# The samples' second small product of a pair is put behind the next pair's sums, in the same PSUM bank

## The chip, the cores and the metric

The kernel runs on one core of one Trainium2 chip. The metric is the device time in microseconds (us) of one execution; lower is better. Three runs of the kernel before the change gave 816.17, 815.36 and 816.26 us, median 816.17 us.

The core's engines run side by side, each through its own list of instructions in order, and wait for each other by semaphores: PE (TensorE, matrix products; its loading of weights is shown as PEld), DVE (VectorE), ACT (ScalarE), POOL (GpSimd), and SP, which only issues DMAs. [...]

## The reference, cut to what matters

One inference step of a hybrid decoder layer: 1024 prompt positions and 8 x 4 = 32 sample positions go through the same weights. `h @ w_in` gives the queries, keys, values and gates of two branches, an mLSTM and a sliding-window attention; these are gated, projected, summed, projected by `w_o` and normalised.

```python
h, gate = adaln_in(x, c, w_ada, b_ada, g_norm)
(mq, mk, mv, mi, mf, mo, mz, aq, ak, av, az, gm, ga) = split_in(h @ w_in)
y_m, C, n, m = mlstm_branch(mq, mk, mv, mi, mf, mo, mz, C0, n0, m0, b_i, b_f, g_mn)
...
o = sink_attend(...)
y_a = o.astype(x.dtype) * jax.nn.silu(az)
u = jax.nn.sigmoid(gm) * (y_m @ w_mo) + jax.nn.sigmoid(ga) * (y_a @ w_ao)
x = x + gate * (u @ w_o)
```

What the change touches is the 32 sample rows of `h @ w_in` for most of these columns.

## The kernel before

**Pairs.** The columns of `w_in` are worked in 20 pairs of 128-column blocks (`pairs`, line 1750): six of the mLSTM heads' queries, keys and values (`head_in`), eight of the merge gates (`gate`), two of the attention's output gate (`query_gate`), four of the mLSTM's (`head_gate`). For the prompt, `block_products` (line 1511) runs seven block products for each pair, 12 matmuls each, of 128x512 float32r elements; each pass writes one of the banks named `bx`, `bw`, `by`, `bz`. Below these are called **fast products**. They fill the stretch from about 128 to 632 us of the span.

**Samples.** For the 32 sample columns, `Pair.samples` (line 1360) multiplies the pair's raw float32 weights with the sample activations `c32`: 16 small float32 matmuls, four side by side in 128x32 tiles of the array (tile `smp`, a bank of the ring `pb`). They leave four partial sums one under the other; ACT copies them to SBUF (`smps`). A second product, `smpo` (line 1377), multiplies `smps` with a constant 0/1 matrix, which sums the parts and turns rows into columns: 128x64, in the full 128x128 tile. What follows is by kind: two DVE copies into `qs`, `ks`, `vs` for `head_in`, a tanh on ACT (`gts`), with DVE work behind it for two kinds, and DMAs to DRAM for the others.

**Turns.** All other float32 work (the attention's scores `sc`, transposes `pt` and outputs `oT`, the mLSTM's `S`, `U`, `n`, the sample heads) is done by generators that `Side` (line 113) steps in between the fast products. `Side.tick` is called after each three fast products; it counts time in `now` by a cost per matmul. A generator yields a lag and the PSUM rings it will need: a step waits for its lag, then for a turn. A turn is opened when two steps are ripe and their banks free by the plan, or one has been late by 4.0, and 2.0 have passed since the last. `take` marks a bank of ring `b` as held for 3.5. `samples` takes a bank and opens a turn at once (`side.tick(True)`), which others may join. `samples_end` asked for one with a lag of 3.0, in stream "e".

PE's order is fixed to the order in which the program is written out. In the stretch of the pairs the lists of DVE and ACT are put in order by the framework's scheduler when the program is built, so an instruction there can stand earlier than its place in the text. A PSUM tile of ring `pb` waits until the tile two before it in the ring has been read.

Of the kernel before, what the change touches and what calls it, by code (L numbers as in the profile page):

```python
# [35 lines left out]
C_ID, C_S9, C_TRI, C_CM, C_AM, C_TS, C_CS, C_RS, C_S32, C_BM, C_S64 = 0, 128, 137, 265, 393, 649, 681, 713, 745, 777, 785  # L36
# [152 lines left out]
def body(tc, a):  # L189
    nc = tc.nc  # L190
    with ExitStack() as ctx:
# [5 lines left out]
        def pg(shape, name):  # L197
            return ps.tile(shape, F32, tag="g", bufs=2, name=name)

        def pa(shape, name):  # L200
            return ps.tile(shape, F32, tag="a", bufs=2, name=name)

        def pb(shape, name):
            return ps.tile(shape, F32, tag="b", bufs=2, name=name)

        def po(shape, name):
            return ps.tile(shape, F32, tag="o", bufs=2, name=name)
# [4 lines left out]
        def sm(shape, name, bufs=3, dt=F32):  # L212
            return sp.tile(shape, dt, tag=name, bufs=bufs, name=name)
# [8 lines left out]
        def in_order(ins, eng="PE"):  # L222
            i = getattr(ins, "ins", ins)
            no_sync(i, [last[eng]] if eng in last else [])
            last[eng] = i

        class Ordered:
            def __init__(self, eng, name):
                self.eng, self.name, self.on = eng, name, True
# [11 lines left out]
        V, S, G = Ordered(nc.vector, "V"), Ordered(nc.scalar, "S"), Ordered(nc.gpsimd, "G")  # L241
# [45 lines left out]
        side = Side(stores, {"m": (2, 35.0), "a": (5, 7.0), "x": (2, 0.0), "s": (2, 20.0), "g": (1, 0.0), "e": (2, 0.0)}, 2.0, 4.0)  # L287
        def mm(out, lhsT, rhs, start, stop, share=1, more=False):
            n = int(np.prod(rhs.shape[1:]))
            side.now += max(n, 250) / 2400 if rhs.dtype == F32R else max(n * 4 // share, 128) / 2400  # L290
            side.products += 1
            in_order(nc.tensor.matmul(out, lhsT, rhs, start=start, stop=stop, skip_group_check=more))  # L292
# [38 lines left out]
        cst = cp.tile([128, C_END], F32, name="cst")  # L331
# [20 lines left out]
        c32 = cp.tile([128, KT, 32], F32, name="c32")  # L352
# [207 lines left out]
        ready, loaded = {}, {}  # L560
# [269 lines left out]
        heads_done, samples_done, units_done, products_done = [], [], [], []  # L830
# [490 lines left out]
        def sum_blocks():  # L1321
# [22 lines left out]
                yield 1.5, ""  # L1344
            formed.append("t1")

        class Pair:
            def __init__(self, kind, i):
                self.kind, self.i = kind, i
# [9 lines left out]

            def samples(self):  # L1360
                side.take("b")
                acc = pb([128, 128], "smp")
                for k in range(4):
                    for j in range(4):
                        mm(acc[32 * j:32 * j + 32], c32[:, 4 * (j % 2) + k], self.raw[j // 2, j % 2][:, k],
                           start=(k == 0), stop=(k == 3), share=4)
                self.sums = sm([128, 128], "smps", 2)
                S.copy(self.sums, acc)
                side.add("e", self.samples_end())
                side.tick(True)  # L1370

            def samples_end(self):
                while self.kind is head_gate and len(samples_done) < self.i + 2:
                    yield 1.0, ""
                yield 3.0, "b"
                o = pb([128, 64], "smpo")
                mm(o, self.sums, cst[:, C_S64:C_S64 + 64], start=True, stop=True)
                self.kind.samples(self, o.rearrange("p (c s) -> p c s", c=2))

            def first_sums(self):  # L1380
                self.raw["s1"] = raw_tile("ws1")
# [246 lines left out]
        def first_split(n, i, eng):  # L1628
# [30 lines left out]
        acc = [(pg([128, 384], "g_ak0"), po([128, 384], "g_av0")),  # L1659
               (po([128, 384], "g_ak1"), pg([128, 384], "g_av1")),  # L1660
               (pa([128, 384], "g_ak2"), pa([128, 384], "g_av2"))]
# [88 lines left out]
        pairs = [Pair(head_in, i) for i in range(len(paired))] + [Pair(gate, d) for d in range(KT)] + [Pair(query_gate, i) for i in range(2)] + [Pair(head_gate, h) for h in range(NH)]  # L1750
# [179 lines left out]
        v, e, y, w = (sm([128, 1], f"fl{i}", 1) for i in range(4))  # L1930
# [189 lines left out]
def build(d):  # L2120
    nc = bacc.Bacc("TRN2", target_bir_lowering=False, num_devices=1, dynamic_dma_scratch_size=4096)
    aps = {}
    for k, v in d.items():
        aps[k] = nc.dram_tensor(k, v.shape, mybir.dt.from_np(v.dtype), kind="ExternalInput").ap()
    for k, s in OUTS.items():
        aps[k] = nc.dram_tensor(k, s, F32, kind="ExternalOutput").ap()
    with tile.TileContext(nc) as tc:
        body(tc, aps)
    return nc
# [19 lines left out]
```

## Time and profile before

| what | value |
|---|---|
| median of three runs | 816.17 us (815.36 to 816.26) |
| the profiled execution's own time | 816.73 us |
| its span, first to last instruction | 814.9 us |
| mean granted TensorE clock | 0.998 |
| DVE busy | 601.2 us (74%), 1631 instructions |
| ACT busy | 409.2 us (50%), 996 instructions |
| POOL busy | 105.3 us (13%), 196 instructions |

Busy time is the time in which an engine has an instruction in work. The chain is the work that ended last, followed back from the last instruction to the first. In the timeline a row has its start, its length, the engine, the line, the operation, what it writes and reads, the shape, and the number of instructions that it stands for; in brackets, how long the engine had been idle and what ended that. A matmul's length has its way through the array in it; the distance from one start to the next is what PE spends. One float32 matmul is two records.

### The profile page before, as it was taken

The numbers are of one execution on the slowest core, as the hardware profiler recorded it, in microseconds if no ns is written. First come the engines' busy times: TensorE is split into PE (matmuls) and PEld (weight loads), VectorE is DVE, ScalarE is ACT, GpSimd is POOL, SyncE is SP. The second block draws the span as 40 slices with busy tenths as digits, with TensorE's granted clock in tenths as the row PEclk, the third lists the DMA queues.
The fourth block names the chain that finished last, engine by engine and source line by source line (L and its number), as shares of the span: only waits on it lengthen the run. The fifth ranks groups of instructions, "written<-read, shape, count | busy, mean of one in ns | idle before, by whom it ended". The sixth has DMA issues, their size and how long they took to land.

```text
span 814.9 us, 15087 instructions
## 1 busy us (share of the span) xinstructions
PE 795.6 (98%) x5071; PEld 650.3 (80%) x5071; DVE 601.2 (74%) x1631; ACT 409.2 (50%) x996; POOL 105.3 (13%) x196
## 2 busy tenths in 40 slices
PE   6899999999999999999999999999999999999996
PEld 2688887777777767887888888787788999997785
DVE  3789747989776866665766787899786677767576
ACT  4674243655646757645454655564545244215344
POOL 0220000222222220010211110111101100000041
PEclk9999999999999999999999999999999999999999
DMA  9977646878785475744364675573455698534532
GB/s 322 373 228 203 177 125 223 265 228 238 249 249 168 115 220 171 226 135 150 101 184 133 184 188 172 160 210 91 138 169 185 227 346 305 173 102 167 204 110 104
DMA packets 111041, 157.26 MB, mean 193 GB/s; under 512 B 19712, under 2 KB 61440, under 8 KB 110932
## 3 DMA queue, kind: packets, MB, share of 16 engines
q1 hardware_dynamic: 96148, 135.58, 52.5%
q10 hardware_dynamic: 11232, 14.42, 5.0%
q0 software_dynamic: 3584, 6.30, 3.9%
q8 instruction: 40, 0.66, 0.4%
q14 instruction: 37, 0.30, 0.1%
HBM read 112.58 MB, written 44.69 MB: 193 GB/s over the span
## 4 chain that ended last, share of the span: by engine, by line
PE 93%; DVE 2%; DMA 2%; ACT 1%; issue 1%; SPq 0%; ACTq 0%; DVEq 0%
PE bw L292 14%; PE by L292 13%; PE bx L292 13%; PE bz L292 7%; PE g_aq L292 6%; PE g_w_mo L292 6%; PE g_w_ao L292 5%; PE foX L292 3%; PE foW L292 2%; PE smp L292 2%; PE foY L292 2%; PE sc L292 2%; PE oT L292 2%; PE n L292 2%; PE g_ak L292 1%; PE g_av L292 1%
## 5 line engine op out<-in xcount | busy, mean ns | idle before, releaser
L273 POOL DMA_DIRECT2D yhD<-yt x48 | 28.8, 607 | 230.9 <-DVE yt L235 139.6
L292 PE MATMUL g_w_ao<-ya,wh_w_ao 128*128 128x384 f32 (+1 forms) x192 | 45.7, 322 | 0.1
L292 PE MATMUL g_w_mo<-ym_l,wh_w_mo 128*128 128x384 f32 (+1 forms) x192 | 45.7, 323 | 0.0
L235 ACT ACTIVATE p<-p,nmx 128x256 f32<-128x256 f32 (+1 forms) x64 | 31.0, 486 | 21.4 <-DVE nmx L235 20.7
L273 POOL DMA_DIRECT2D mkN<-mkt x32 | 20.9, 659 | 133.5 <-DVE p L235 71.8
L292 PEld LDWEIGHTS g_w_ao<-ya,wh_w_ao 128*128 128x128 f32 x192 | 33.5, 188 | 0.7 <-DVE ya L235 0.6
L292 PEld LDWEIGHTS g_w_mo<-ym_l,wh_w_mo 128*128 128x128 f32 x192 | 33.5, 188 | 0.0
L292 PE MATMUL g_aq<-h_h,wh_aq 128*128 128x384 f32 (+1 forms) x96 | 31.9, 333 | 0.0
L292 PE MATMUL g_aq<-h_l,wh_aq 128*128 128x384 f32 (+1 forms) x96 | 31.0, 323 | 0.0
L292 PE MATMUL g_w_mo<-ym_l,wl_w_mo 128*128 128x384 f32 (+1 forms) x96 | 31.0, 323 | 0.0
L292 PE MATMUL g_aq<-h_h,wl_aq 128*128 128x384 f32 (+1 forms) x96 | 31.0, 323 | 0.0
L292 PE MATMUL g_w_ao<-ya,wl_w_ao 128*128 128x384 f32 (+1 forms) x96 | 30.8, 321 | 0.0
L235 ACT CAST uwh<-u_h 128x512 fp32r<-128x512 f32 x27 | 16.6, 620 | 27.3 <-PE foY L292 10.5
L235 DVE TENSOR_TENSOR uwl<-u_h,uwh 128x512 fp32r<-128x512 f32 x27 | 18.5, 689 | 12.5 <-ACT uwh L235 12.4
L235 DVE CUSTOM_DVE_ANT_0 p<-sc,cst,sink 128x256 f32<-128x256 f32 (+1 forms) x64 | 26.1, 461 | 1.0 <-PE sc L292 1.0
L273 POOL DMA_DIRECT2D mvN<-mvt x32 | 20.7, 653 | 37.3 <-DVE mvt L235 36.3
L235 ACT CAST wo_h<-wo_l 128x512 fp32r<-128x512 f32 x28 | 17.1, 620 | 13.8 <-DVE u_h L235 10.6
L235 POOL TENSOR_TENSOR fr_w<-fr_y 128x2 f32<-128x2 f32 (+1 forms) x12 | 3.5, 291 | 144.2 <-DVE fr_y L235 143.6
L235 ACT ACTIVATE p<-p,den 128x128 f32<-128x128 f32 x56 | 18.6, 394 | 5.1 <-DVE den L235 4.5
L235 DVE TENSOR_TENSOR wo_l<-wo_l,wo_h 128x512 fp32r<-128x512 f32 x28 | 18.7, 686 | 2.5 <-ACT wo_h L235 2.4
L235 DVE SCALAR_TENSOR_TENSOR p<-p,den 128x128 f32<-128x128 f32 x56 | 17.3, 345 | 4.2 <-ACT wh_pgate__3658 L235 2.9
L292 PEld LDWEIGHTS g_aq<-h_h,wh_aq 128*128 128x128 f32 x96 | 18.0, 188 | 2.7 <-issue 2.5
(1621 smaller groups left out, 2684.3 us busy)
## 6 DMA issues: line engine op xcount, KB each, us to landing
x<-xT SPq DMA_DIRECT2D x16, 256.0 KB
early_h<-w_ada SPq DMA_DIRECT2D x8, 512.0 KB
adar_ga<-w_ada SPq DMA_DIRECT2D x16, 256.0 KB
ow<-w_out SPq DMA_DIRECT2D x16, 256.0 KB
woD_t<-ow SPq DMA_DIRECT2D x16, 256.0 KB
wr_ga<-w SPq DMA_DIRECT2D x16, 256.0 KB
wr_gm<-w SPq DMA_DIRECT2D x16, 256.0 KB
taD<-gt ACTq DMA_DIRECT2D x16, 256.0 KB
```

The lines of the kernel that those rows point to most:

```text
L235: ins = f(*args, **kw)
L273: nc.gpsimd.dma_start(out, in_)
L292: in_order(nc.tensor.matmul(out, lhsT, rhs, start=start, stop=stop, skip_group_check=more))
```

## The change

`samples` no longer hands its second product to a stream. It leaves the pair in a list, `pending`; the next pair's `samples`, right behind its own 16 matmuls, issues the second product of the pair before it into columns 128 to 191 of its own bank, then the copy of its own sums, then the former pair's evacuation from those columns. A `head_gate` pair whose sample head is not yet done, and the last pair of all, still go through `samples_end`, with a lag of 0.0 in place of 3.0.

```diff
+        pending = []
...
             def samples(self):
                 side.take("b")
-                acc = pb([128, 128], "smp")
+                acc = pb([128, 192], "smp")
                 for k in range(4):
                     for j in range(4):
-                        mm(acc[32 * j:32 * j + 32], c32[:, 4 * (j % 2) + k], self.raw[j // 2, j % 2][:, k],
+                        mm(acc[32 * j:32 * j + 32, 0:128], c32[:, 4 * (j % 2) + k], self.raw[j // 2, j % 2][:, k],
                            start=(k == 0), stop=(k == 3), share=4)
+                now = [p for p in pending if p.ready()]
+                for p in now:
+                    p.turn(acc[:, 128:192])
                 self.sums = sm([128, 128], "smps", 2)
-                S.copy(self.sums, acc)
-                side.add("e", self.samples_end())
+                S.copy(self.sums, acc[:, 0:128])
+                for p in pending:
+                    if p in now:
+                        p.evac_samples(acc[:, 128:192])
+                    else:
+                        side.add("e", p.samples_end())
+                pending[:] = [self]
+                if self is pairs[-1]:
+                    side.add("e", pending.pop().samples_end())
                 side.tick(True)
 
+            def ready(self):
+                return self.kind is not head_gate or len(samples_done) >= self.i + 2
+
+            def turn(self, o):
+                mm(o, self.sums, cst[:, C_S64:C_S64 + 64], start=True, stop=True)
+
+            def evac_samples(self, o):
+                self.kind.samples(self, o.rearrange("p (c s) -> p c s", c=2))
+
             def samples_end(self):
-                while self.kind is head_gate and len(samples_done) < self.i + 2:
+                while not self.ready():
                     yield 1.0, ""
-                yield 3.0, "b"
+                yield 0.0, "b"
                 o = pb([128, 64], "smpo")
-                mm(o, self.sums, cst[:, C_S64:C_S64 + 64], start=True, stop=True)
-                self.kind.samples(self, o.rearrange("p (c s) -> p c s", c=2))
+                self.turn(o)
+                self.evac_samples(o)
```

**On PE, at the second pair.** Before, the first pair's second product stands alone between fast products:

```order
L292 MATMUL bx<-h_l_585,wh_phead_in_2__1516 128x512
L292 MATMUL bx<-h_h_584,wl_phead_in_2__1517 128x512
L292 MATMUL smpo<-cst,smps 128x64
L292 MATMUL bx<-h_h_584,wh_phead_in_2__1516 128x512
L292 MATMUL bx<-h_l_585,wh_phead_in_2__1516 128x512
```

and a little later the second pair's sums (the last two of 16 are shown) are followed at once by an attention step's scores:

```order
L292 MATMUL smp<-wr_mq_0_1512,c_106 32x128
L292 MATMUL smp<-wr_mq_1_1514,c_106 32x128
L292 MATMUL sc_0_0_1650<-ukv,uqv 128x128
L292 MATMUL sc_0_1_1651<-ukv,uqv 128x128
L292 MATMUL sc_0_0_1650<-ukv,uqv 128x256
L292 MATMUL sc_0_1_1651<-ukv,uqv 128x256
```

Now, in the changed kernel, at the same sums:

```order
L292 MATMUL smp<-wr_mq_0_1512,c_106 32x128
L292 MATMUL smp<-wr_mq_1_1514,c_106 32x128
L292 MATMUL smp<-cst,smps 128x64
L292 MATMUL sc_0_0_1649<-ukv,uqv 128x128
L292 MATMUL sc_0_1_1650<-ukv,uqv 128x128
L292 MATMUL sc_0_0_1649<-ukv,uqv 128x256
```

The lone product is gone from among the `bx` rows, and the same product, in the full tile, stands between the sums (128x32 tiles) and the scores (64x128 tiles).

Over the stretch of the pairs the order has 80 turns of small work before and 81 after (counted from the first pair's second product on). Second products: 20 before, 6 of them alone in a turn; 18 of 20 right behind sums after, one alone, one with a sample head's transpose at the very end. Turns with nothing else in them: of scores 0 before and 6 after, of transposes `pt` 1 and 5, of outputs `oT` 0 and 4. Places at which one small-tile kind of the attention or the sums follows another directly (`smp` then `sc`, `sc` and `oT` either way): 9 before, 3 after; in 4 more after, the second product stands between.

**On PE, at the sums of the second merge-gate pair.** Before, the last small work ahead of these sums is a turn with the transposes `pt`, and 15 fast products stand between; the last ones and the first sums are:

```order
L292 MATMUL bx<-h_l_585,wh_pgate_2__3443 128x512
L292 MATMUL bx<-h_h_584,wl_pgate_2__3444 128x512
L292 MATMUL smp<-wr_ga_0_3435,c_106 32x128
L292 MATMUL smp<-wr_ga_1_3437,c_106 32x128
L292 MATMUL smp<-wr_gm_0_3439,c_106 32x128
```

Now an attention step's outputs `oT`, in a bank of the same ring, stand three fast products ahead of them:

```order
L292 MATMUL oT_4_3498<-p_3211,uqv 64x128 x2
L292 MATMUL oT_4_3498<-p_3210,uqv 64x128 x2
L292 MATMUL bx<-h_h_584,wh_pgate_2__3370 128x512
L292 MATMUL bx<-h_l_585,wh_pgate_2__3370 128x512
L292 MATMUL bx<-h_h_584,wl_pgate_2__3371 128x512
L292 MATMUL smp<-wr_ga_0_3362,c_106 32x128
L292 MATMUL smp<-wr_ga_1_3364,c_106 32x128
```

The turn with `oT` has moved close to the sums.

**On DVE, at an evacuation of a `head_in` pair.** `wl`, `wr` and `mkv` are work for the fast products, `ISA` is the fused addition of mask and row maximum that empties `sc`; in brackets is what a row waits for. Before:

```order
L235 TENSOR_TENSOR wl_phead_in_6__2129<-wr_mk_0_1833,wh_phead_in_6__2128 128x512 [waits PE_49,Activation_49]
L235 COPY ks<-smpo 128x32 [waits PE_49]
L235 COPY vs<-smpo 128x32
L235 TENSOR_TENSOR ow_1891<-ow_1891,ow_1897 128x512 [waits DMAHW5_49,DVE_49]
L235 TENSOR_TENSOR ow_1895<-ow_1895,ow_1891 128x512 [waits DMAHW2_49,DVE_49]
```

Now:

```order
L235 STREAM_TRANSPOSE mkt<-mkv 128x512 [waits Activation_49]
L235 TENSOR_TENSOR wr_mk_0_2141<-wr_mq_0_2137,wr_mk_0_2141 128x512 [waits PE_49]
L235 COPY ks<-smp 128x32 [waits Activation_49]
L235 COPY vs<-smp 128x32
L235 ISA p_2281,mx<-sc_0_0_2284,cst,sink 128x128 [waits PE_49]
```

The copies used to wait for PE; now they wait for ACT's copy of the new pair's sums from the same bank, and the emptying of the scores stands behind them.

## The prediction

> **What bounds the kernel now.** I read the page first: the span, PE's busy time and the chain that ended last.
>
> ```profile
> span 814.9 us, 15087 instructions
> PE 795.6 (98%) x5071; PEld 650.3 (80%) x5071; DVE 601.2 (74%) x1631; ACT 409.2 (50%) x996; POOL 105.3 (13%) x196
> PE 93%; DVE 2%; DMA 2%; ACT 1%; issue 1%; SPq 0%; ACTq 0%; DVEq 0%
> ```
>
> PE is the bound: it is busy for 98% of the span and carries 93% of the chain. So the change is worth what it changes in PE's own time, plus what it changes in the moments at which PE stands still. The second view is that of PE's waits; in the stretch of the pairs (128 to 632 us) one wait stands out:
>
> ```profile
> PE pt L297 <- DVE mx L235: 2.3, 1, 2.3
> ```
>
> The third view is the timeline of PE around the second products. All of them together are this group (two records each):
>
> ```profile
> L292 PE MATMUL smpo<-cst,smps x40: 217/275/323, 134.3 to 629.8; 128*128 128x64 f32 x40
> ```
>
> **What a second product costs, alone and in company.** From one start to the next, a fast product takes 0.23 us. Here is one second product alone between fast ones, then one behind four transposes, then four transposes without it:
>
> ```profile
> 134.12 0.39 PE L292 MATMUL bx<-h_h,wl_phead_in__1517 128*128 128x512 f32 x1
> 134.35 0.33 PE L292 MATMUL smpo<-cst,smps 128*128 128x64 f32 x2
> 134.49 0.47 PE L292 MATMUL bx<-h_h,wh_phead_in__1516 128*128 128x512 f32 x1
> 134.80 0.39 PE L292 MATMUL bx<-h_l,wh_phead_in__1516 128*128 128x512 f32 x1
> ...
> 273.31 0.39 PE L292 MATMUL by<-t3l,wh_phead_in__3136 128*128 128x512 f32 x1
> 273.54 0.40 PE L292 MATMUL by<-t3h,wl_phead_in__3137 128*128 128x512 f32 x1
> 273.77 0.60 PE L297 MATMUL pt<-cst,p 128*128 128x128 f32 x4
> 274.21 0.33 PE L292 MATMUL smpo<-cst,smps 128*128 128x64 f32 x2
> 274.35 0.48 PE L292 MATMUL bx<-h_h,wh_pgate__3176 128*128 128x512 f32 x1
> 274.67 0.40 PE L292 MATMUL bx<-h_l,wh_pgate__3176 128*128 128x512 f32 x1
> ...
> 327.55 0.39 PE L292 MATMUL bx<-h_h,wl_pgate__3807 128*128 128x512 f32 x1
> 327.78 0.60 PE L297 MATMUL pt<-cst,p 128*128 128x128 f32 x4
> 328.14 0.48 PE L292 MATMUL bx<-h_h,wh_pgate__3806 128*128 128x512 f32 x1
> 328.45 0.39 PE L292 MATMUL bx<-h_l,wh_pgate__3806 128*128 128x512 f32 x1
> ```
>
> I take each turn from the last fast product before it to the second one after it, less two fast products (0.46). Alone: 134.80 - 134.12 - 0.46 = 0.22 us. In company: (274.67 - 273.54 - 0.46) - (328.45 - 327.55 - 0.46) = 0.67 - 0.44 = 0.23 us. A turn of its own costs this product nothing extra, because it runs in the same full tile as the fast products. So the 6 lone turns that go (of 20) save **0.0 us**; all 20 products stay, some 4.4 us before and after. No row shows the product behind `smp`. The bounds: 0.14, its own two starts (274.21 to 274.35), if the way back to fast products is paid already by the sums, and 0.22, if not. I take 0.22, the same in both rows with other neighbours.
>
> **What the neighbours lose.** The other small work has been regrouped, and tile shapes matter there:
>
> ```profile
> 329.38 0.40 PE L292 MATMUL bx<-h_h,wl_pgate__3807 128*128 128x512 f32 x1
> 330.71 0.50 PE L292 MATMUL by<-t3h,wh_pgate__3827 128*128 128x512 f32 x1
> 331.05 0.40 PE L292 MATMUL by<-t3l,wh_pgate__3827 128*128 128x512 f32 x1
> ...
> 268.51 0.40 PE L292 MATMUL bx<-h_h,wl_phead_in__3092 128*128 128x512 f32 x1
> 269.85 1.14 PE L292 MATMUL sc<-ukv,uqv 64*128 64x256 f32 x8
> 270.91 0.50 PE L292 MATMUL by<-t3h,wh_phead_in__3136 128*128 128x512 f32 x1
> 271.25 0.40 PE L292 MATMUL by<-t3l,wh_phead_in__3136 128*128 128x512 f32 x1
> ...
> 201.47 0.40 PE L292 MATMUL bw<-h_h,wl_phead_in__2320 128*128 128x512 f32 x1
> 201.80 1.13 PE L292 MATMUL sc<-ukv,uqv 64*128 64x256 f32 x8
> 203.59 0.39 PE L292 MATMUL by<-t4l,wh_phead_in__2355 128*128 128x512 f32 x1
> ```
>
> Between 329.38 and 330.71 stand the sums alone: 331.05 - 329.38 - 0.46 = 1.21 us. With scores directly behind them it is 271.25 - 268.51 - 0.46 = 2.28, so scores add 1.07. In a turn with full-tile transposes (the last three rows) it is 203.59 - 201.47 - 0.46 = 1.66, less 0.44 for the transposes 1.22. Scores that go from the full tile and back to it thus cost **0.15 us** more than scores that follow another small tile, which save one change of shape. By the order, such direct contacts fall from 9 to 3: 6 x 0.15 = **+0.9 us**. Joins of equal tiles are two before and two after. Bounds: nothing, and 6 x 0.33, the whole step from the fast product at 268.51 into the first `smp` at 268.84, so 2.0.
>
> [...]
>
> **Where PE stands still.** The 2.3 us wait, in detail:
>
> ```profile
> 303.21 0.88 PE L292 MATMUL oT<-p,uqv 128*64 128x128 f32 x12
> 306.35 0.66 PE L297 MATMUL pt<-cst,p 128*128 128x128 f32 x4 [2.26 <-DVE mx L235]
> ...
> 300.98 0.56 DVE L235 TENSOR_TENSOR et<-et,cst 128x384 f32<-128x384 f32 x1 [1.06 <-DMA et<-nmd]
> 304.60 0.48 DVE L235 CUSTOM_DVE_ANT_0 p<-sc,cst,sink 128x256 f32<-128x256 f32 x1
> ```
>
> DVE waited for a DMA of the first mLSTM head, fell behind, and began only at 304.60 to empty the scores of an earlier turn, four such instructions; the transposes wanted that bank. It is an encounter of one attention step with the first head's load. The regrouping moves all turns there, and whether they meet again cannot be read from the order. I take it that this encounter goes (**-2.3 us**); the bounds are -2.3 and 0. Late next is then the bank in which the outputs `oT` stand three fast products ahead of sums:
>
> ```profile
> 171.42 1.09 PE L292 MATMUL oT<-p,uqv 128*64 128x128 f32 x16
> 172.44 0.43 PE L292 MATMUL smpo<-cst,smps 128*128 128x64 f32 x2
> 172.56 0.37 ACT L235 COPY ukv<-oT 128x256 f32<-128x256 f32 x1 [0.65 <-PE oT L292]
> 251.45 0.62 ACT L235 CAST wh_phead_in__3054<-wr_mk 128x512 fp32r<-128x512 f32 x1 [0.40 <-PE smpo L292]
> ```
>
> What follows `oT` starts at 172.44 and ACT has emptied the bank at 172.93. Three fast products take 0.34 + 0.23 + 0.33 = 0.90, to 173.34: no wait if ACT is idle, 0.2 with one cast of 0.62 in front of its copy, 0.8 with two. I take **+0.3**, bounds 0 and 0.8.
>
> The rest I cost at nothing.
>
> ```profile
> L292 PE MATMUL sS<-qs,ks x8: 196/206/217, 458.9 to 572.7; 128*32 128x32 f32 x8
> ```
>
> The evacuations come a pair later, but on PE `qs`, `ks` and `vs` are read by the sample heads alone, from 458.9 on, long after the last `head_in` pair; the gates' columns, stored to DRAM through ACT's and SP's queues, are read in the output stage. That cover is gone only for the last pair, whose product now stands at the end of the stretch, at the same 0.22. The ring `pb` has 18 tiles fewer to hand round, which can only ease it; against that, sums hold their bank until DVE or ACT has read the other columns too.
>
> **Sum.** The profiled execution took 816.73 us: 816.73 + 0.0 + 0.9 - 2.3 + 0.3 = 815.6. It lies 0.56 above the median of the runs, 816.17, against which the change is measured: **815.1 us**.
>
> **Rivals.**
>
> *The product is cheaper behind the sums.* If it costs 0.14 there, 18 x 0.08 = 1.4 us go: 813.7, and 812.8 if the changes of shape cost nothing. For it: the way out of a small tile is paid once per turn, 0.34 at 330.71. Against it: `oT` is a small tile too, and behind it (172.44) the product took 0.25 until the next fast one. 813.4, chance 0.16.
>
> *The encounter comes back,* or one like it elsewhere: DVE is busy 74% of the span, and its order has no room made for a late DMA. 815.1 + 2.3 = 817.4, chance 0.22. With this, the change doesn't do what it says, for the lone turns it saves were free.
>
> *Slower: a bank that two engines share chains DVE to ACT.* Six `head_in` evacuations on DVE now wait for ACT's copy of the new sums, with the emptying of scores queued behind them.
>
> ```profile
> L292 PE MATMUL smp<-wr_mv,c x64: 272/273/297, 138.1 to 243.5; 128*32 128x128 f32 x64
> 246.64 0.25 ACT L235 COPY smps<-smp 128x128 f32<-128x128 f32 x1
> ```
>
> Here ACT came to the copy 3.1 us after the last sum, behind the attention's exponentials. DVE would stand until 246.89. The plan holds a bank for 3.5 and emptying the scores takes 4 x 0.48 = 1.9, so it decides once the copy ends over 1.6 us late and DVE has nothing else to do before it. If that falls on two of the six, at 2.26 each by the row at 306.35, it is 815.1 + 4.5 = 819.6. Against it: the copy waits for the same products as the evacuation, so an idle ACT costs DVE some 0.3 us. Chance 0.18.
>
> [...]
>
> **Chances and range.** The forecast has 0.44, its own range 814.0 to 816.5. 0.2% is 1.6 us, about what a measurement can tell from no change, so the bounds are 814.5 and 817.8. Faster: 0.16 of the cheap product and 0.15 of the forecast, 0.31. Slower: 0.16 of the chained DVE and 0.06 of the returned wait, 0.22. The same: 0.47. The range is 812.8 to 819.4: from the cheap product with free changes of shape nearly to the middle of the slower case, whose upper half is left out.
>
> **What would show it.** Right: the starts from the last `smp` across the product to the second fast one lie 0.22 above those at 329.38 to 331.05; no wait of `pt` for `mx` in the list of PE's waits; PE's busy time within 2 us of 795.6 plus or minus the wait. The cheap product: 0.14 there. The chain: DVE rows of `qs`, `ks`, `vs` with idle time ended by ACT's `smps`, and after them PE waiting for DVE. What would make the forecast wrong most easily is another encounter of DVE's queue with a late DMA or a late ACT, which the order doesn't tell.

## The result, and the profile after

| | median | range, runs |
|---|---|---|
| before | 816.17 us | 815.36 to 816.42, 5 |
| after | 823.55 us | 822.13 to 824.33, 5 |

The changed kernel is slower: ratio 1.0094, 95% interval 1.0080 to 1.0107. That is 7.4 us, where 1.1 us of gain had been predicted, and it lies above the range. The profiled execution took 822.13 us, the fastest of the five. Its page:

```profile
span 820.3 us, 15093 instructions
PE 798.7 (97%) x5071; PEld 651.5 (79%) x5071; DVE 598.2 (73%) x1631; ACT 408.9 (50%) x996; POOL 105.1 (13%) x196
PE 89%; DMA 4%; DVE 3%; ACT 1%; issue 1%; SPq 0%; ACTq 0%; DVEq 0%
```

The span is 5.4 us longer with the same 5071 records on PE. In the chain (last line) PE has fallen from 93% to 89%, and DMA has risen from 2% to 4%. The list of PE's waits no longer has the 2.3 us of `pt` for `mx`; it has a longer one:

```profile
PE fq L297 <- DVE p L235: 3.3, 1, 3.3
```

The timeline of PE at that place (start, length, what is written and read):

```profile
159.50 0.39 PE L292 MATMUL bw<-t2h,wl_phead_in__1778 128*128 128x512 f32 x1
163.18 0.20 PE L297 MATMUL fq<-cst,gt 4*32 4x4 f32 x2 [3.29 <-DVE p L235]
...
165.18 0.63 PE L292 MATMUL bx<-h_h,wh_phead_in__1829 128*128 128x512 f32 x1
165.61 0.63 PE L292 MATMUL bx<-h_l,wh_phead_in__1829 128*128 128x512 f32 x1
```

`fq` is a small transpose of the mLSTM's gates. Its bank still holds the `pt` of an attention step, which DVE has not read. Behind the standstill fast products start 0.43 us apart (165.18 to 165.61) instead of 0.23. The stretches show why; the columns are the busy time of PE, PEld, DVE, ACT and POOL, then the granted clock, the DMA engines' share and GB/s:

```profile
160.00:165.00 5.00, 1.82 (x8) 1.53 (x9) 3.40 (x15) 2.36 (x7) 0.00 (x0) 0.93 0.88 304
165.00:170.00 5.00, 5.00 (x53) 3.47 (x52) 4.01 (x16) 3.43 (x13) 0.93 (x2) 0.73 0.29 104
```

The clock was 0.93 and 0.73 (0.50 from 164.4 to 167.6 us): 5 x 0.07 + 5 x 0.27 = 1.7 us lost, besides the 3.3. So one encounter costs 5.0 us. What DVE did meanwhile:

```profile
161.56 0.69 DVE L235 TENSOR_TENSOR ws<-wr_mv,wr_mv 128x512 f32<-128x512 f32 x1 [6.38 <-DMA wr_mv<-w]
...
162.46 0.66 DVE L235 TENSOR_TENSOR p<-pt,cst 128x512 f32<-128x512 f32 x1
```

DVE stood 6.4 us at `ws`, the first sum of the next pair's raw weights, until a load of `wr_mv` had landed. `p<-pt`, which empties the bank that PE wants, was queued behind it. In the kernel before it ran ahead of `ws`, and `ws` had no wait:

```profile
156.72 0.65 DVE L235 TENSOR_TENSOR p<-pt,cst 128x512 f32<-128x512 f32 x1
...
158.08 0.67 DVE L235 TENSOR_TENSOR ws<-wr_mv,wr_mv 128x512 f32<-128x512 f32 x1
```

Why the weights came late is in SP's list (start, time to issue, what is moved), first of the kernel before, here and three pairs of loads later:

```profile
145.68 3.04 SPq L277 DMA_DIRECT2D woD_t<-ow  x4
...
149.92 0.89 SPq L277 DMA_DIRECT2D wr_mk<-w  x2
150.90 0.86 SPq L277 DMA_DIRECT2D wr_mv<-w  x2
...
231.87 0.93 SPq L277 DMA_DIRECT2D wr_mk<-w  x2
232.89 0.98 SPq L277 DMA_DIRECT2D wr_mv<-w  x2
235.51 2.24 SPq L277 DMA_DIRECT2D woD_t<-ow  x3
```

and of the changed kernel, at the same two places:

```profile
147.69 0.32 SPq L277 DMA_DIRECT2D kD<-mkv  x1
150.41 0.32 SPq L277 DMA_DIRECT2D woD_t<-ow  x1
150.82 2.14 SPq L277 DMA_DIRECT2D wr_mk<-w  x2
153.05 3.71 SPq L277 DMA_DIRECT2D wr_mv<-w  x2
...
235.41 2.25 SPq L277 DMA_DIRECT2D woD_t<-ow  x3
...
238.79 0.93 SPq L277 DMA_DIRECT2D wr_mk<-w  x2
239.76 1.03 SPq L277 DMA_DIRECT2D wr_mv<-w  x2
```

`woD_t` are stores of folded output-projection weights (`out_weights`, line 1233 of the changed kernel); each must wait until DVE has formed it. At the first place four of them stand ahead of the loads in both kernels. Before, the last is out by 148.72. After the change the last goes out only at 150.41, when DVE has formed it, and SP, idle since 148.0, can't issue the loads behind it sooner. They begin 0.9 us later than before (150.82 for 149.92), although PE is 0.6 us ahead there (the second pair's sums start at 137.48 for 138.10). Then SP takes up to 3.71 us over two of them instead of 0.86, so that the last is out at 156.76 instead of 151.76. At the second place one store stood ahead of the loads and three behind; now three stand ahead, at 235.41, and the loads follow at 238.79 instead of 231.87. Of these 6.9 us, PE's own lateness is 2.4 (the sums of the pair before start at 219.00 for 216.59). PE feels that second lateness itself, in the sums:

```profile
244.41 0.40 PE L292 MATMUL bx<-h_h,wl_phead_in__2769 128*128 128x512 f32 x1
244.74 0.41 PE L292 MATMUL smp<-wr_mk,c 128*32 128x128 f32 x4
245.27 0.41 PE L292 MATMUL smp<-wr_mv,c 128*32 128x128 f32 x2
...
247.56 0.49 PE L292 MATMUL by<-t3h,wh_phead_in__2799 128*128 128x512 f32 x1
247.88 0.40 PE L292 MATMUL by<-t3l,wh_phead_in__2799 128*128 128x512 f32 x1
```

Taken as in the prediction, this turn costs 247.88 - 244.41 - 0.46 = 3.01 us. Sums with the product are 1.43 (below) and transposes 0.44, so 1.1 us are waits for weights. (The list of waits has only 0.3 of it, since the longer rows cover the rest. In the run with early loads, below, the same turn takes 1.82, 1.2 less.)

The account of the two spans: -2.3 (the old wait) + 3.3 (`fq`) + 1.7 (half clock) + 1.1 (sums) = 3.8. To the 5.4 measured 1.6 us are missing. The list of waits has 0.8 more than before (`bw` for ACT 1.2 instead of 0.7, `bx` for `zt` 0.3), and the 0.9 forecast for the changes of shape would be the rest; this split is argued, not shown. The account is of one execution each. The medians lie 7.4 us apart; the three slowest of the five have a mean granted clock of 0.993, the profiled one 0.995, and 0.002 of 820 us is 1.6 us. By this estimate most of the further 2 us is more time at the lower clock, in executions that left no trace.

### The profile page after: what moved, and what is told of

Its sections match the earlier page's. It is cut to its first block, busy times and chain, and to the rows that moved or that the text cites. A ratio compares the mean times of both kernels' runs of the same rounds, so it can differ in the third digit from the quotient of the medians.

```text
span 820.3 us, 15093 instructions
## 1 busy us (share of the span) xinstructions
PE 798.7 (97%) x5071; PEld 651.5 (79%) x5071; DVE 598.2 (73%) x1631; ACT 408.9 (50%) x996; POOL 105.1 (13%) x196
## 4 chain that ended last, share of the span: by engine, by line
PE 89%; DMA 4%; DVE 3%; ACT 1%; issue 1%; SPq 0%; ACTq 0%; DVEq 0%
PE by L292 13%; PE bx L292 13%; PE bw L292 12%; PE bz L292 6%; PE g_aq L292 6%; PE g_w_mo L292 6%; PE g_w_ao L292 6%; PE smp L292 3%; PE foX L292 3%; PE foW L292 2%; PE foY L292 2%; PE oT L292 2%; PE n L292 2%; DMA wr_mv<-w 1%; PE g_ak L292 1%; PE sc L292 1%
## 5 line engine op out<-in xcount | busy, mean ns | idle before, releaser
L235 DVE TENSOR_TENSOR h_l<-x,h_h 128x512 fp32r<-128x512 f32 x20 | 13.7, 692 | 7.2 <-ACT h_h L235 5.9
```

The source lines that it names most:

```text
L235: ins = f(*args, **kw)
```

## The experiments

Twelve kernels, each timed in five rounds beside the kernel before on the same chip. All ratios below are against that.

**Which part of the change costs the time? The joining alone.** The product is joined to the sums as in the change, except for the four `head_gate` pairs, which keep a turn of their own as before. The planner keeps its books as before: a step without a product takes the old turn, with its bank and its time on the clock (these are the main lines of the edit). All other products stand where they stood before.

```diff
+                clock = side.now, side.products
                 for p in now:
                     p.turn(acc[:, 128:192])
+                side.now, side.products = clock
...
+            def turn_kept(self):
+                yield 3.0, "b"
+                side.now += max(64 * 4, 128) / 2400
+                side.products += 1
```

> The product stays joined to the next pair's sums and in their bank, but the planner still counts the old turn for it, so that all other work on PE stands exactly in the order of before. Regrouping theory (the loss comes from where the other turns went, above all the place where DVE's list has the next pair's weight sum, waiting for a late DMA, ahead of the emptying of banks): 814.5 to 817.5 us, PE's 3.3 us wait of fq gone. Shared-bank theory (DVE chained to ACT's copy by the common bank): 820 or more. Product theory (the product is dearer behind the sums): 16 joins at some 0.1 to 0.3 more, 818 to 821.

Measured: 817.15 us, 1.0011 (0.9999 to 1.0023). So the joined product and the shared bank cost next to nothing, and the loss comes with the new places of the other turns. (SP's loads near 150 us begin late here too, at 152.67, and are out by 154.99; DVE's `ws` waits 3.0 us for them, and PE has no wait for `fq`.)

**The product in a bank of its own,** with PE's order of the change:

```diff
-                acc = pb([128, 192], "smp")
+                acc = pb([128, 128], "smp")
...
+                own = pb([128, 64], "smpo") if now else None
                 for p in now:
-                    p.turn(acc[:, 128:192])
+                    p.turn(own)
```

> As the changed kernel, with the same order on PE, but the product goes into a bank of its own, so that DVE doesn't wait for ACT's copy of the sums. Regrouping theory: still slow, 821 to 825 us, with a DVE wait for the weights' DMA of several us. Shared-bank theory: 815 to 818.

Measured: 835.13 us, 1.0233 (1.0208 to 1.0258), worse by far and outside what either theory had said. The longest in its list of PE's waits:

```profile
PE fq L297 <- DVE p L235: 3.0, 1, 3.0
PE sc L292 <- ACT smps L235: 2.8, 1, 2.8
PE sU L292 <- ACT smps L235: 2.3, 1, 2.3
PE pt L297 <- ACT smps L235: 2.3, 1, 2.3
```

The wait of `fq` is still there, without the shared bank. The program has its PSUM tiles in four rings of two buffers (`bufs=2`); a second place in ring `pb` made the next small work wait, three times (2.8, 2.3 and 2.3 us), until ACT had copied the sums (`smps`). The shared bank was not the harm; it avoids these three waits.

**Was it the place of `ws` in DVE's list?** An order edge keeps the sum of raw weights behind the matmul that stands ahead of it in the program, in the changed kernel and, as control, in the kernel before.

```diff
-                V.tensor_tensor(self.raw["s1"], self.raw[1, 0], self.raw[1, 1], op=ALU.add)
+                ins = V.tensor_tensor(self.raw["s1"], self.raw[1, 0], self.raw[1, 1], op=ALU.add)
+                if "PE" in last:
+                    no_sync(getattr(ins, "ins", ins), [last["PE"]])
```

> The changed kernel, with one more order edge: the first sum of the next pair's raw weights (ws) may not be put ahead of the matmul that precedes it in the program, so DVE cannot stand at it early while banks wait to be emptied. PE's order is unchanged. Regrouping theory: the 3.3 us wait of fq and the 3.4 us at half clock behind it (1.7 us lost) go, 823.55 - 5.0 = 818.5 us or less, clock 0.998. Shared-bank theory: 822 or more.

> The kernel before with the same order edge. It tells whether the edge is worth something by itself. Regrouping theory: DVE's list of before had no such long wait (1.3 us at most for weights), so 815 to 817 us; if the edge alone gave more than 2 us, e3 could not be read as the undoing of the change's loss.

Measured: after with the edge 823.21 us, 1.0081 (1.0066 to 1.0097); before with the edge 817.16, 1.0007 (0.9995 to 1.0019). The edge did what it was made for, and the time hardly moved. (By its bound alone, 822 or more, this would speak for the shared bank; the two runs above rule that out.) Waits of PE in the changed kernel with the edge:

```profile
PE smp L292 <- DMA wr_mv<-w: 1.5, 2, 0.9
PE fq L297 <- DVE mx L235: 1.4, 1, 1.4
PE bx L292 <- DVE zt L235: 0.9, 1, 0.9
PE smp L292 <- DMA wr_mk<-w: 0.6, 1, 0.6
```

In the profiled execution, the fastest of six, the 3.3 us and the half clock were gone, but the sums now waited 2.1 us for weights. This theory fell: DVE's order only decided where the lateness came out, not whether. That led to the weights themselves.

**The weights earlier,** by one block of twelve products, with PE's program unchanged, in the changed kernel and in the kernel before:

```diff
-                if i == (5 if n else 1) and nxt:
+                if (n, i) == (0, 1) and nxt:
                     nxt.load()
+                if i == 4 and n + 2 < len(jobs):
+                    jobs[n + 2].load()
```

> The changed kernel, with the raw weights of every pair from the third on asked for one block of twelve products earlier; TensorE's program is the changed kernel's own, product by product. Theory A: the changed kernel loses because the regrouped turns let SP's stores of the output projection's folded weights come ahead of the loads of the next pair's weights (in the trace: the loads for one pair issued at 238.7 us with the edge of the third run, 231.9 before; for another at 150.8 and 153.1, 149.9 and 150.9 before), so that VectorE's sums of raw weights and TensorE's samples' sums stand for a DMA, and what waits for VectorE stands too. Then VectorE's 6.4 us wait for wr_mv, TensorE's 3.3 us wait for fq's bank, the half clock behind it and the waits of the samples' sums for weights near 245 us all go or fall under half a microsecond each: 817 to 819 us, since what is left is the contacts of unlike tiles and the small waits near 425 and 509. Theory B: the order of TensorE's products itself costs the time (contacts of unlike tiles, refills), and loads matter little: 821.5 to 823.5 us.

> The kernel before with the same earlier loads, as the control for the run on the changed kernel. TensorE never stands for a weight load there, and VectorE's waits for raw weights are 1.1 us in all, so both theories say 816.4 within 0.8 us. Were it as much faster as the changed kernel becomes by the same edit, the edit would have a worth of its own and would say nothing about the change.

Measured: after with early loads 816.7 us, 1.0001 (0.9986 to 1.0015); before with early loads 818.97, 1.0024 (1.0009 to 1.0039). The whole loss is gone, and not because early loads are good by themselves: they harm the kernel before a little, 2.0 us, where no change had been expected. The page, SP's list and DVE's timeline of the changed kernel with early loads:

```profile
span 814.6 us, 15115 instructions
```

```profile
148.80 0.88 SPq L277 DMA_DIRECT2D wr_mk<-w  x2
149.77 0.86 SPq L277 DMA_DIRECT2D wr_mv<-w  x2
151.11 0.33 SPq L277 DMA_DIRECT2D woD_t<-ow  x1
```

```profile
155.73 0.68 DVE L235 TENSOR_TENSOR ws<-wr_mv,wr_mv 128x512 f32<-128x512 f32 x1
160.41 0.69 DVE L235 TENSOR_TENSOR p<-pt,cst 128x512 f32<-128x512 f32 x1
```

`ws` still stands ahead of `p<-pt`, now without a wait. The last of the four stores is behind the loads, the other three ahead of them. But these loads are earlier as well, so a further run separates the two.

**The stores behind the loads,** the loads left in place, in the changed kernel (`store` of `woD_t` passes `"wr"`, which sets `behind`):

```diff
+        def issue(out, in_, late=False, near=False, behind=False):
...
             if near:
                 no_sync(ins, [last["PE"]])
+                last["wr"] = ins
+            if behind:
+                no_sync(ins, [last["wr"]])
```

> The changed kernel; the loads of raw weights stay where the change has them, but the four stores of folded output weights (woD_t) may not come ahead of the last loads of raw weights on SP. TensorE's program is the changed kernel's own. Theory A1: the loads are late because they stand on SP behind stores that wait for VectorE; then this alone takes back what the earlier loads took back: 815.5 to 818.5 us, no half clock before the end, and VectorE's longest wait for wr_mv under 3 us. Theory A2: the loads lack lead whatever stands ahead of them, and the earlier loads helped by the 3 us of one block; then 820.5 to 823.5 us.

Measured: 817.62 us, 1.0012 (1.0003 to 1.0022). So the order on SP alone gives back all but about 1 us of the loss. Its SP list at the same place:

```profile
150.74 0.87 SPq L277 DMA_DIRECT2D wr_mk<-w  x2
151.70 0.86 SPq L277 DMA_DIRECT2D wr_mv<-w  x2
152.61 8.83 SPq L277 DMA_DIRECT2D woD_t<-ow  x4
```

All four stores are behind the loads now, not only the last, so the run doesn't tell which of them matters. The profiled execution, the slowest of the eleven (819.01 us), runs 1.9 us late from before the pairs on (the second pair's sums start at 139.36, in the changed kernel at 137.48). Counted from these sums the loads begin after 11.4 us, in the changed kernel after 13.3 and in the kernel before after 11.8. They take SP 0.87 and 0.86 us instead of 2.14 and 3.71, so the last is out after 13.2 instead of 19.3. So of the 6.1 us that the loads are late in the changed kernel, 2.0 are the late start, where SP stood for the last store, and 4.1 the slow issue. The stores now need 8.8 us from the first to the last, their waits for DVE included, and nothing on PE waits for them. DVE's longest wait for `wr_mv` is 2.4 us, as expected. No half clock was expected either, and where the changed kernel has it there is none (1.00 from 160 to 170 us); but the clock falls ahead of the pairs, to 0.84 from 65 to 70 us and 0.81 from 70 to 75, which costs 5 x 0.16 + 5 x 0.19 = 1.7 us there.

**The weights later, in the kernel before,** by one block, as the counterpart:

```diff
-                if i == (5 if n else 1) and nxt:
+                if i == (6 if n else 1) and nxt:
                     nxt.load()
```

> The kernel before with the raw weights of every pair but the first two asked for one block of twelve products later (about 3 us); TensorE's program is unchanged. If late weights are what costs the changed kernel its time (theory A), the kernel before must lose by them too: VectorE's sums and the samples' sums wait for DMAs in many of the pairs, with TensorE standing 0.5 to 3 us at several: 820 to 840 us. If the loads have more lead than that, TensorE shows no such wait and it stays within 1 us of 816.5; then lateness by the 2 to 7 us seen in the changed kernel could not be the whole cause.

Measured: 826.54 us, 1.0124 (1.0105 to 1.0144). PE's waits in it:

```profile
PE pt L297 <- DVE mx L235: 2.8, 1, 2.8
PE smp L292 <- DMA wr_gm<-w: 1.8, 3, 0.8
PE smp L292 <- DMA wr_mz<-w: 1.6, 4, 0.8
```

The first row is the old wait of 2.3 us, grown; the others are new. They show a part of the 10 us only. The kernel before has less than one block, about 3 us, of lead to lose. Its time rested on it, and no wait on PE showed that. DVE's list did hint at it: in the kernel before `ws` waits 6.0 us in all for raw weights, at most 1.3 at a time. (The expectation for early loads in the kernel before has 1.1 in all; that is `wr_mv` alone.)

**Is it this regrouping, or any?** Two kernels change the plan alone. In the changed kernel the planner books the old turn again, with its bank and its place, but without a product and without time on its clock; in the kernel before the lone product becomes due after 4 us instead of 3.

```diff
+                if self.kind is not head_gate:
+                    side.add("e", self.place())
...
+            def place(self):
+                yield 3.0, "b"
```

```diff
-                yield 3.0, "b"
+                yield 4.0, "b"
                 o = pb([128, 64], "smpo")
```

> The changed kernel, but the planner still books the turn that the change took away (3 us after the sums, one place of the ring of PSUM banks, a partner for other small turns), without any product in it and without time on the planner's clock; the product stays joined to the sums. TensorE's order then differs from before's in 589 of 4119 places, against 1923 in the changed kernel. Theory C: the loss comes from the booking that went, because other turns grouped with it; then this comes out near the run that kept the plan whole, 815.5 to 818.5 us. Theory D: what counts is when the planner's clock counts the product; then it stays near the changed kernel, 821 to 824 us.

> The kernel before, with nothing joined: only the lone product becomes due 4 us after its sums in the planner instead of 3, which moves 1337 of the 4119 products to other places. Theory E: any regrouping of the small turns of this size moves the time by its own encounters (a bank not yet empty, a weight not yet landed), up or down, without the join; then it leaves 816.4 by more than 1.2 us to either side, and the waits that TensorE shows then are other ones than those of the kernel before. Rival: only the join's own way of grouping harms; then it is within 1.2 us of 816.4.

Measured: with the place booked 818.77 us, 1.0016 (0.9997 to 1.0035), so most of the loss goes with the booking that went: other turns were grouped by it. It is just above the bound set for that, so the clock's share isn't settled. With 4 us 826.34, 1.0109 (1.0086 to 1.0132): a regrouping without any join costs more than the change. It has its own encounter, seen in the list of PE's waits:

```profile
PE bx L292 <- DVE zt L235: 4.6, 1, 4.6
```

and on DVE ahead of that `zt`:

```profile
507.28 0.56 DVE L235 TENSOR_TENSOR qw<-qw,hq 128x384 f32<-128x384 f32 x1 [1.20 <-DMA qw<-wid]
508.26 0.69 DVE L235 SCALAR_TENSOR_TENSOR zt<-zt,bx 128x512 f32<-128x512 f32 x1 [0.42 <-ACT zt L235]
```

Again an instruction that empties a bank stands behind one that waits for a DMA; of the 4.6 us, 1.2 are that wait. What the other 3.4 are was not followed further. The clock drops behind this standstill too (0.93 from 505 to 510 us, 0.73 from 510 to 515).

**Does a version beat both?** Two candidates: early loads with the edge in the changed kernel, and early loads with the plan kept.

> The changed kernel with the earlier loads and with the edge of the third run (VectorE's sum of raw weights not ahead of the product that stands before it in the program): does a version come out that beats both kernels? With the earlier loads TensorE's only waits over half a microsecond between 130 us and the end of the pairs are one of 0.8 at 420 us; the edge has nothing left to save but VectorE's places, so 815.5 to 817.5 us, not told from the earlier loads alone. A time under 814.5 would mean that the hoisted sum costs something that the list of TensorE's waits does not show.

> The run that kept the planner's books as before and joined the product, with the earlier loads added: the other candidate for a version that beats both. The earlier loads cost the kernel before 0.24% by new small waits of pt for VectorE's maxima; those stand in the same places here, so 816 to 819 us. Under 814.5 would say that join and early loads add up to a gain.

Measured: 816.34 us, 0.9994 (0.9985 to 1.0003), and 817.41, 1.0009 (1.0000 to 1.0018). Neither beats the kernel before. With nothing late, the change is worth nothing that can be measured.

## Why the prediction was wrong, point by point

- *A lone turn costs the product nothing extra, and behind sums it costs 0.22.* Right. (Of the 6 lone turns, the trace of before has four alone between fast products, at 134.35, 388.50, 413.77 and 629.79; two more stand beside `sU`. At 0.0 each this changes nothing.) In the changed kernel sums with the product, alone between fast products, run like this:

```profile
330.88 0.40 PE L292 MATMUL bx<-h_h,wl_pgate__3729 128*128 128x512 f32 x1
...
332.46 0.48 PE L292 MATMUL by<-t3h,wh_pgate__3767 128*128 128x512 f32 x1
332.77 0.39 PE L292 MATMUL by<-t3l,wh_pgate__3767 128*128 128x512 f32 x1
```

  332.77 - 330.88 - 0.46 = 1.43, against 1.21 without the product: 0.22. The rival "cheaper behind the sums" fell.
- *The neighbours lose +0.9.* The step holds; its sum comes out somewhat smaller. Eight scores alone between fast products, which the kernel before has nowhere, cost 278.11 - 276.39 - 0.46 = 1.26 us in the changed kernel, against 1.07 directly behind sums: 0.19, where 0.15 was taken. And the second pair's sums with their scores cost 2.06 before and 2.43 with the product between them: 0.22 for the product and 0.15 for the lost contact. Summed the prediction's way over all small turns of the stretch, the run with early loads has 116.5 us, the kernel before 118.3 with the 2.3 us wait and 116.0 without it: +0.5.
- *The encounter at 303 to 306 us goes, -2.3, and the bounds are -2.3 and 0.* This is the step that failed. That wait did go. But the upper bound 0 says that the regrouping brings back at most the same wait, and what stands still was followed for PE, DVE and ACT, never for SP. There the loads of raw weights, on which both DVE's sums and PE's `smp` live, stand behind stores that wait for DVE. The regrouping made these stores late against the loads, and the loads came late with them: 3.3 + 1.7 + 1.1 = 6.1 us in the account. SP's order alone would not have told it: at the first place the four stores stand ahead of the loads before as after, and only at the second have two more moved ahead.
- *Sums behind `oT` wait, +0.3.* Wrong, small: the sums that follow `oT` so closely, near 302 us, cost 1.44, as sums with the product alone do elsewhere, so no wait.
- *The rival "the encounter comes back, or one like it elsewhere"* had the right kind (DVE at a late DMA, a bank not emptied behind it) and the wrong size, since it was given the 2.3 us of the one known case.
- *The slower rival, a shared bank that chains DVE to ACT,* fell. With the old plan (the four `head_gate` pairs apart) the shared bank costs 0.11% (-0.01 to 0.23), and a bank of its own with the new plan 2.3%.
- *The cover of moved evacuations* held: PE has no wait for `qs`, `ks`, `vs` or the gates' columns.

With early loads the changed kernel comes near to what the sum had said: the ratio 1.0001 (0.9986 to 1.0015) against 0.9987 forecast, just inside the interval, and the span 0.3 us shorter than before, where the sum has 1.1. The sum had the right terms for PE and none for the time at which SP can issue the loads.

## What to carry to other kernels

Where a planner places work by its own clock, taking out one step moves others. Look on every queue, the one that only issues DMAs too, for loads that stand behind stores which wait for an engine: here they were as late as the last of these (the store at 150.41, the loads from 150.82 on), though the order at that place had not changed. That PE showed no wait for weights said nothing here on how much lead stood behind it (one block of about 3 us less cost 10 us); shift the load by one step and measure. And once a stall appears, ask for its source: moving the waiting instruction alone put the lateness in another place (the 3.3 us at `fq` went, and the sums waited 2.1).

## What the runs showed of the hardware that was not expected

A standstill of PE cost half its own length again and more, where the granted clock dropped behind it: 1.7 us on top of 3.3 in the changed kernel, at 0.93 and 0.73. In the kernel before, a wait of 2.26 us was followed by full clock (1.00 to 315 us). In the run with a bank of its own one of 2.3 us (`pt`) was followed by half clock, as was one of 2.8 in the kernel with late loads, and the 3.3 us one above. The stretches with or behind the wait, of the first three in that order (the column ahead of the last two is the clock):

```profile
305.00:310.00 5.00, 3.65 (x18) 2.84 (x20) 2.46 (x13) 3.47 (x13) 0.00 (x0) 1.00 0.08 29
```

```profile
255.00:260.00 5.00, 5.00 (x20) 3.73 (x21) 3.08 (x8) 0.96 (x2) 2.06 (x4) 0.66 0.35 52
```

```profile
310.00:315.00 5.00, 5.00 (x20) 3.50 (x19) 1.61 (x7) 4.55 (x16) 0.00 (x0) 0.70 0.24 82
```

0.66 and 0.70 over 5 us are 1.7 and 1.5 us lost. The 2.8 us wait of `sc` with a bank of its own lost twice as much: 0.80 and 0.51 in the two stretches from 195 to 205 us, 5 x 0.20 + 5 x 0.49 = 3.5 us. So waits of 2.3 and 2.8 us were enough here, and two of nearly the same length differed: 2.26 us with 1.00 behind it, 2.3 with 0.66. Nor was a standstill always there: in the profiled execution with the stores behind the loads products of `g_aq` start 0.27 to 0.33 us apart from 68.42 to 71.88 us, and 0.17 to 0.19 behind that, at the clocks of 0.84 and 0.81 given above. The timeline has no wait of PE there, and the kernel before has 1.00 from 65 to 75 us. What set that off stays open.

The time that SP takes to issue a load is not constant: 0.43 each in the kernel before and with the stores behind (0.86 for two), 1.86 each in the changed kernel (3.71 for two). What sets it wasn't tried by itself; it is the larger part of the lateness near 150 us, 4.1 of 6.1 against the run with the stores behind, and went with the order of stores and loads. With early loads there are slow issues as well, but they fall on the loads `ow` behind the weights: the four take 6.46 us, from 153.65 on, where in the changed kernel the four take 2.72, from 157.79 on.
